# Scaling the normalised input by its rows' factors once, in place, instead of scaling the results of its projections

## Chip, core and metric

The kernel runs on one core of one Trainium2 chip. A core has TensorE (PE, the matrix engine), VectorE (DVE), ScalarE (ACT), GpSimd (POOL) and SyncE (SP, which here issues the transfers); each works through its own queue in order, and they wait for each other at semaphores. PE's results go into the banks of PSUM, 128 partitions by 512 fp32 numbers each. The metric is the device time of one execution in microseconds.

## What is computed

One layer of a decoder trunk, with 512 rows of 1024 numbers. The part that the change touches is the first norm, the projection behind it and what the projection's parts go through first:

```python
u = rms_norm(h, norm_mix_pre[l])        # h * rsqrt(mean(h*h) + EPS) * gain, row by row
proj = jnp.einsum("btd,dp->btp", u, w_in[l])
(a_x, a_gate, p_x, c_q, c_f, c_i, c_g, s_b, s_c, s_x,
 gate_logits) = jnp.split(proj, split_points, axis=-1)
y_a = rg_lru_branch(a_x, a_gate, ...)   # convolution, real-gated linear recurrence
y_b = pool_branch(p_x, ...)             # causal mean pooling over windows 2, 4, 8, 16
y_c = hgrn2_branch(c_q, c_f, c_i, c_g, ...)   # f = lb + (1 - lb) * sigmoid(c_f)
y_d = short_conv_branch(s_b, s_c, s_x, ...)   # s_b * conv3(s_c * s_x)
gates = jax.nn.sigmoid(gate_logits.reshape(bsz, t, N_BRANCHES, D_MODEL))
merged = jnp.sum(gates * branch_out, axis=2)
```

After it come an output projection, a second norm, a squared-ReLU MLP (1024 to 4096 and back) and a last norm.

## The kernel before

The input stands transposed: features on the 128 partitions, the 512 rows along the free axis, eight slices of features (k = 0 to 7). Every fp32 matmul is made of three in the format fp32r: each operand is split into a high part (ACT copies it into fp32r, L167) and a low part (DVE subtracts the high part, L168). The splits of the weights are the tiles whi and wlo (128x1024 each), those of the input uh and ul. `mm3` (L237 to L240) issues the three products: L238 high by high, L239 and L240 the mixed ones.

A slot is 256 columns of the combined projection: ten for the mixers (in the order s_c and s_x, s_b, p_x, c_f, c_q, c_i, c_g, a_x, a_gate) and 16 for the gates. `slot_mm` takes two PSUM banks and issues 48 matmuls of 128x512 into them; a unit of weights lasts for half a slot, and the weights of later units are loaded and split four units ahead, into a few buffers that come free as the matmuls that read them are done. c_i alone is computed the other way round, with rows on the partitions, in matmuls of 128x256.

The norm's gains are in uh and ul already (L266, L271). The rows' factors, 1/sqrt(mean square + EPS), are not: they are known later than PE can start. They stand along the free axis in `rstd_bc` (128x512, made on PE and copied at L371), and once more with rows on the partitions in `rst4`. So every result that leaves PSUM is multiplied by them on DVE:

```python
def evac(dst, ps):
    return dve.tensor_tensor(dst, ps, rstd_bc, ALU.mult)   # L387 is its line in the trace
```

There are 50 such products: 18 for the mixers' slots, 32 for the gates', whose sigmoid (L779) follows in place. In the names of the trace, mm and sm are banks of PSUM, t and s working tiles. The work around the change:

- s_c, s_x and s_b: product of the first two (L410), a convolution of three taps (L420, L422), times s_b (L423), split into yhi and ylo.
- p_x: the mean pooling, some ten steps on DVE (L433 to L443); its result is split (ACT's copy `t<-t` at L167, DVE's subtraction at L168), and a product with a block-diagonal matrix bd_h, bd_l follows on PE (`sm<-t,bd_h`, the pool product).
- c_f: two products, then on ACT the sigmoids of z and of -z (L466, L467).
- The first branch's gates run beside the recurrence of branch A (L560 to L597), whose functions on ACT are other ones than sigmoid; a change of function table is an ACT_TABLE_LOAD there.
- Much later a second norm's rows are transposed on PE (L910) and split into u2h and u2l, and the up projection reads them (ub).

The order of each engine's instructions isn't that of the code: a scheduler sets it when the kernel is built, except for those that the code pins. So an edit in one place can move instructions in others.

Of the kernel before, what the change touches and what calls it, by code (L numbers as in the profile page):

```python
# [9 lines left out]
F32R = mybir.dt.float32r  # L10
I32 = mybir.dt.int32
U8 = mybir.dt.uint8
AF = mybir.ActivationFunctionType
ALU = mybir.AluOpType

P = 128
T = 512
# [4 lines left out]
W = 256  # L22
# [5 lines left out]
PAD = 16  # L28
# [21 lines left out]
def tile_hybrid_trunk(ctx: ExitStack, tc: tile.TileContext, x0, xT, xn, wts, dn, par, bd, cst, msk, gains, out):  # L50
    nc = tc.nc
    act, dve, pool, pe = nc.scalar, nc.vector, nc.gpsimd, nc.tensor

    cp = ctx.enter_context(tc.tile_pool(name="cp", bufs=1))
    up = ctx.enter_context(tc.tile_pool(name="up", bufs=4))
# [6 lines left out]
    yp = mix.enter_context(tc.tile_pool(name="yp", bufs=8))  # L62
# [10 lines left out]
    def nm(s):  # L73
        cnt[0] += 1
        return f"{s}_{cnt[0]}"

    def t_tile(dt=F32):
        return tp.tile([P, 2 * TP], dt, tag="t", name=nm("t"))

    def t_full(dt=F32):  # L80
        return t_tile(dt)[:, : 2 * T].rearrange("p (c t) -> p c t", c=2)

    def t_pad():
        return t_tile().rearrange("p (c t) -> p c t", c=2)

    def s_tile(n=T):
        return sp.tile([P, T], F32, tag="s", name=nm("s"))[:, :n]

    def mm_bank():
        return mp.tile([P, T], F32, tag="mm", name=nm("mm"))  # L90
# [4 lines left out]
    def y_pair():  # L95
        r = []
        for s in ("hi", "lo"):
            r.append(yp.tile([P, 2 * T], F32R, tag="y", name=nm("y" + s)))
        return r
# [7 lines left out]
    rstd_bc = cx_.tile([P, T], F32, name="rstd_bc")  # L107
    sbd = cx_.tile([P, 3, 2, P], F32, name="sbd")
    rst4 = cp.tile([P, NT], F32, name="rst4")
# [8 lines left out]
    x0t = cx_.tile([P, T + NK], F32, name="x0t")  # L118
    xt = [ap_.tile([P, 2, T], F32, tag="acc", name=nm("xt")) for _ in range(4)]
# [46 lines left out]
    def split(hi, lo, src, pin=False):  # L166
        a_ = act.activation(hi, src, AF.Copy)  # L167
        d_ = dve.tensor_tensor(lo, src, hi.bitcast(F32), ALU.subtract)  # L168
        if pin:
            K(a_)  # L170
            K(d_)
# [59 lines left out]
    def unit():  # L231
        i = use[0]
        use[0] += 1
        prep(i + ahead[0])
        return Wt.hl.pop(i)

    def mm3(ps, lh, ll, rh, rl, first, last):  # L237
        pe.matmul(ps, lh, rh, start=first, stop=False)  # L238
        pe.matmul(ps, lh, rl, start=False, stop=False)  # L239
        pe.matmul(ps, ll, rh, start=False, stop=last)  # L240
# [10 lines left out]
            dve.tensor_tensor(t, t, h, ALU.mult)  # L251
            dve.scalar_tensor_tensor(y, t, 1.5, y, ALU.add, ALU.mult)

    uh = [up.tile([P, 4, T], F32R, tag="u", name=nm("uh")) for _ in range(2)]
    ul = [up.tile([P, 4, T], F32R, tag="u", name=nm("ul")) for _ in range(2)]

    def U(lst, k, a=0, b=T):
        return lst[k // 4][:, k % 4, a:b]

    def xhi(k):  # L260
        src = x0t[:, :T] if k == 0 else xt[k // 2][:, k % 2]
        g = x0t[:, T + k : T + k + 1]
        if k == 0:
            dve.tensor_scalar(U(uh, k), src, g, None, ALU.mult)
        else:
            act.activation(U(uh, k), src, AF.Copy, scale=g)  # L266
# [40 lines left out]
    for k in range(NK):  # L307
        pair = (0, 1) if k < 4 else (2, 3)
        if k in CUTS:
            o, e = CUTS[k]  # L310
# [62 lines left out]
    def slot_mm(bank=mm_bank, mid=None):  # L373
        bs = [bank(), bank()]
        for h in range(2):
            if h == 1 and mid:
                mid()
            wh, wl = unit()
            for kk in range(4):
                k = 4 * h + kk  # L380
                for c in range(2):
                    o = kk * W + c * P
                    mm3(bs[c], wh[:, o : o + P], wl[:, o : o + P], U(uh, k), U(ul, k), k == 0, k == NK - 1)
        return bs

    def evac(dst, ps):
        return dve.tensor_tensor(dst, ps, rstd_bc, ALU.mult)  # L387

    def emit_y(y):
        hi, lo = y_pair()  # L390
        split(hi, lo, y.rearrange("p c t -> p (c t)"))
        return (hi.rearrange("p (c t) -> p c t", c=2), lo.rearrange("p (c t) -> p c t", c=2))
# [13 lines left out]
            K(evac(sx[:, c], b1[c]))  # L406

    b2 = slot_mm(sm_bank, first_evacs)
    for c in range(2):
        dve.tensor_tensor(cx[:, c, PAD:], cx[:, c, PAD:], sx[:, c], ALU.mult)  # L410
    sb = t_full()
# [3 lines left out]
    for c in range(2):  # L415
        for j in range(SCONV):
            src = cx[:, c, PAD - (SCONV - 1) + j : PAD - (SCONV - 1) + j + T]
# [5 lines left out]
    dve.tensor_tensor(cv, cv, sb, ALU.mult)  # L423
    ys[3] = emit_y(cv)

    bs = slot_mm()
    px = t_pad()
    for c in range(2):
        dve.memset(px[:, c, :PAD], 0.0)
# [9 lines left out]
    o, _ = PAR["corr"]  # L439
# [20 lines left out]
    bs = slot_mm()  # L460
    f = t_full()
    kk_ = t_full()
    for c in range(2):
        z = s_tile()
        evac(z, bs[c])
        act.activation(f[:, c], z, AF.Sigmoid)  # L466
        act.activation(kk_[:, c], z, AF.Sigmoid, scale=-1.0)  # L467
        dve.tensor_scalar(f[:, c], f[:, c], omlb[:, c : c + 1], lb[:, c : c + 1], ALU.mult, ALU.add)
        dve.tensor_scalar(kk_[:, c], kk_[:, c], omlb[:, c : c + 1], None, ALU.mult)
    hi, lo = y_pair()  # L470
# [8 lines left out]
    bs = slot_mm()  # L479
    q = t_full()  # L480
    for c in range(2):
        evac(q[:, c], bs[c])
    vz = cx_.tile([P, NT, 2, 192], F32, name="vz")
    pool.memset(vz, 0.0)
    v = vz.rearrange("p c k (b e) -> p c k b e", e=64)[:, :, :, 0:3:2]
    uv = [unit(), unit()]
    for t in range(NT):
        if t % 2 == 0:
            vb = mm_bank()
        o = (t % 2) * W  # L490
        for k in range(NK):
            wh, wl = uv[k // 4]
            cs = slice((k % 4) * W, (k % 4) * W + W)
            mm3(vb[:, o : o + W], U(uh, k, t * P, t * P + P), U(ul, k, t * P, t * P + P),
                wh[:, cs], wl[:, cs], k == 0, k == NK - 1)
        if t % 2 == 1:
            for tt in (t - 1, t):
                dve.tensor_scalar(v[:, tt], vb[:, (tt % 2) * W : (tt % 2) * W + W].rearrange(
                    "p (k b e) -> p k b e", b=2, e=64), rst4[:, tt : tt + 1], None, ALU.mult)
    bs = slot_mm()  # L500
    sg = t_full()
    for c in range(2):
        z = s_tile()
        evac(z, bs[c])
        act.activation(sg[:, c], z, AF.Sigmoid)
        dve.tensor_tensor(sg[:, c], sg[:, c], z, ALU.mult)

    bs = slot_mm()
    ax = t_pad()
    for c in range(2):  # L510
        dve.memset(ax[:, c, :PAD], 0.0)
        evac(ax[:, c, PAD:], bs[c])
    bs = slot_mm()
    ag = t_full()
    for c in range(2):
        evac(ag[:, c], bs[c])

    ysA = y_pair()
    sTt = [yp.tile([P, 2 * T], F32, tag="y", name=nm("sT")) for _ in range(2)]
# [229 lines left out]
    def drain(*gens):  # L749
        for g in gens:  # L750
            for _ in g:
                pass
# [4 lines left out]
    def step(g):  # L757
        return next(g, True) is None
# [3 lines left out]
    def accv(d):  # L762
        return acc[d // 2][:, d % 2]

    merged = [None] * 4
    for gi, k in enumerate(GATE_ORDER):
        if gi == 2:
            drain(lru)
        if gi == 3:
            drain(hg)  # L770
        yh, yl = ys[k]
        for dh in range(2):
            gt = []
            for j in range(2):
                bs = slot_mm()
                for c in range(2):
                    g = s_tile()
                    evac(g, bs[c])
                    act.activation(g, g, AF.Sigmoid)  # L779
                    gt.append(g)  # L780
                    if gi == 0:
                        step(lru)
                    else:
                        step(hg)
                        step(hg)
                if j == 1:
                    wh, wl = unit()
                    wq = (wh, wl)
            for d4 in range(4):
                d = 4 * dh + d4  # L790
                pb = mm_bank()
                for c in range(2):
                    o = c * T + d4 * P
                    mm3(pb, wq[0][:, o : o + P], wq[1][:, o : o + P], yh[:, c], yl[:, c], c == 0, c == 1)
                if gi == 0:
                    dve.tensor_tensor(accv(d), pb, gt[d4], ALU.mult)
                else:
                    dve.tensor_tensor(gt[d4], pb, gt[d4], ALU.mult)
                    dve.tensor_tensor(accv(d), accv(d), gt[d4], ALU.add)
                if gi == 3:  # L800
                    if d % 2 == 0:
                        merged[d // 2] = y_pair()
                    mh, ml = merged[d // 2]
                    cs = slice((d % 2) * T, (d % 2) * T + T)
                    split(mh[:, cs], ml[:, cs], accv(d))
# [21 lines left out]
    for ku in range(4):  # L827
        wh, wl = unit()
        for kk in range(2):
            k = 2 * ku + kk  # L830
# [98 lines left out]
    def mid():  # L929
        tb1 = trans(1, mm_bank)  # L930
        for j in range(2):
            put(1, j, tb1[j])
# [341 lines left out]
```

## Time and profile before

| | |
|---|---|
| time, median of 3 runs | 745.71 us (745.67 to 746.75) |
| the profiled execution's own time | 746.69 us |
| its span, from the first to the last instruction | 744.9 us |
| PE busy | 736.8 us, 99% |
| DVE busy | 536.1 us, 72% |
| ACT busy | 312.8 us, 42% |
| mean granted clock of TensorE | 0.997 |

Times are microseconds from the span's start. A row of the timeline is one instruction or several of a kind in a row (x2, x4): start, time from the first's start to the last's end, engine, line, operation, result<-operands without buffer numbers; in brackets the idle time of the engine before it and what ended it. Instructions of one engine overlap a little, so that the next starts before the row's time is over.

### The profile page before, as it was taken

To read this page: it belongs to the slowest core of one execution; us is meant where nothing else is said; L and a number is where in the kernel's file an instruction comes from. 1 tells how busy PE (TensorE), PEld (TensorE's weight loads), DVE (VectorE), ACT (ScalarE), POOL (GpSimd) and SP (SyncE) were. 2 spreads that over 40 slices of the span, in tenths; PEclk is the share of its full clock that TensorE was granted. 3 is DMA by queue.
4 is the path that set the end of the run, shared out by engine and by line. 5 is a ranking of instruction groups with operands and counts; after the bars stand their busy time and mean duration, and the time that the engine had idled before them with its cause. 6 is when DMAs were issued, how large, how long until landed. Compare 5 with 4: busy or idle time off the path is not lost.

```text
span 744.9 us, 8882 instructions
## 1 busy us (share of the span) xinstructions
PE 736.8 (99%) x3506; PEld 620.4 (83%) x3506; DVE 536.1 (72%) x776; ACT 312.8 (42%) x404; POOL 7.2 (1%) x11
## 2 busy tenths in 40 slices
PE   9999999999999999999999999999999999999996
PEld 7888988888888888888888988888888888888885
DVE  6698447559997566554748785788878696976787
ACT  7424223336423322242434566544445362635322
POOL 1100000000000000000000000000000000000000
PEclk9999999999999999999999999999999999999998
DMA  9634232222222353233432614142322315030322
GB/s 333 239 100 154 85 114 85 85 85 85 84 74 97 85 184 127 88 112 94 128 109 94 259 53 170 57 141 86 118 108 90 136 58 170 0 114 29 112 86 113
DMA packets 22761, 84.59 MB, mean 114 GB/s; under 512 B 2624, under 2 KB 3520, under 8 KB 20928
## 3 DMA queue, kind: packets, MB, share of 16 engines
q1 hardware_dynamic: 22288, 83.74, 33.3%
q8 instruction: 27, 0.44, 0.3%
q10 hardware_dynamic: 432, 0.29, 0.1%
q14 instruction: 14, 0.11, 0.1%
HBM read 79.83 MB, written 4.19 MB: 113 GB/s over the span
## 4 chain that ended last, share of the span: by engine, by line
PE 97%; DVE 1%; DMA 0%; ACT 0%; issue 0%; DVEq 0%
PE mm L238 14%; PE mm L240 14%; PE mm L239 14%; PE ub L239 8%; PE ub L238 8%; PE ub L240 8%; PE db L239 6%; PE db L238 6%; PE db L240 6%; PE mm L323 3%; PE sm L612 2%; PE sm L238 2%; PE sm L240 2%; PE sm L239 2%; PE ub L1121 0%; PE ub L1120 0%
## 5 line engine op out<-in xcount | busy, mean ns | idle before, releaser
L167 ACT ACTIVATE whi<-raw 128x1024 fp32r<-128x1024 f32 x98 | 103.7, 1061 | 237.7 <-PE mm L239 109.7
L168 DVE TENSOR_TENSOR wlo<-raw,whi 128x1024 fp32r<-128x1024 f32 x98 | 119.4, 1221 | 75.7 <-ACT whi L167 75.5
L240 PE MATMUL mm<-uh,wlo 128*128 128x512 f32 x352 | 137.2, 390 | 0.0
L239 PE MATMUL mm<-ul,whi 128*128 128x512 f32 x352 | 137.1, 389 | 0.0
L238 PE MATMUL mm<-uh,whi 128*128 128x512 f32 x352 | 136.8, 390 | 0.0
L238 PE MATMUL ub<-u2h,whi 128*128 128x512 f32 (+1 forms) x288 | 105.2, 366 | 0.0
L239 PE MATMUL ub<-u2l,whi 128*128 128x512 f32 (+1 forms) x288 | 105.2, 365 | 0.0
L240 PE MATMUL ub<-u2h,wlo 128*128 128x512 f32 (+1 forms) x288 | 105.2, 365 | 0.0
L240 PEld LDWEIGHTS mm<-uh,wlo 128*128 128x128 f32 x352 | 66.1, 188 | 13.7
L239 PEld LDWEIGHTS mm<-ul,whi 128*128 128x128 f32 x352 | 66.1, 188 | 13.6
L238 PEld LDWEIGHTS mm<-uh,whi 128*128 128x128 f32 x352 | 66.1, 188 | 13.4
L238 PE MATMUL db<-fhi,ahi 128*128 128x512 f32 x196 | 76.2, 389 | 0.0
L239 PE MATMUL db<-flo,ahi 128*128 128x512 f32 x196 | 76.2, 389 | 0.0
L240 PE MATMUL db<-fhi,alo 128*128 128x512 f32 x196 | 76.2, 389 | 0.0
L240 PEld LDWEIGHTS ub<-u2h,wlo 128*128 128x128 f32 x288 | 54.3, 189 | 8.7
L238 PEld LDWEIGHTS ub<-u2h,whi 128*128 128x128 f32 x288 | 54.2, 189 | 8.8
L239 PEld LDWEIGHTS ub<-u2l,whi 128*128 128x128 f32 x288 | 54.3, 189 | 8.7
L1052 DVE TENSOR_TENSOR rows<-rows,db 128x1024 f32<-128x1024 f32 x24 | 29.2, 1217 | 23.3 <-PE db L240 23.3
L167 ACT ACTIVATE fhi<-x 128x1024 fp32r<-128x1024 f32 x28 | 29.6, 1059 | 36.6 <-PE db L240 26.6
L238 PEld LDWEIGHTS db<-fhi,ahi 128*128 128x128 f32 x196 | 36.8, 188 | 7.7
L240 PEld LDWEIGHTS db<-fhi,alo 128*128 128x128 f32 x196 | 36.8, 188 | 7.6
L239 PEld LDWEIGHTS db<-flo,ahi 128*128 128x128 f32 x196 | 36.8, 188 | 7.6
(308 smaller groups left out, 1100.9 us busy)
## 6 DMA issues: line engine op xcount, KB each, us to landing
raw<-in_wts_dram SPq DMA_DIRECT2D x102, 512.0 KB, 3.5
ab<-in_dn_dram SPq DMA_DIRECT2D x14, 1024.0 KB, 4.9
t<-in_xn_dram SPq DMA_DIRECT2D x8, 512.0 KB, 7.4
h1d<-t SPq DMA_DIRECT2D x4, 512.0 KB, 2.6
hr<-h1d SPq DMA_DIRECT2D x2, 1024.0 KB, 6.9
xt<-in_xt_dram SPq DMA_DIRECT2D x7, 256.0 KB, 5.3
out_dram<-mg SPq DMA_DIRECT2D x3, 512.0 KB, 2.6
t<-in_gains_dram SPq DMA_DIRECT2D x2, 512.0 KB, 5.9
```

The lines of the kernel that those rows point to most:

```text
L167: a_ = act.activation(hi, src, AF.Copy)
L168: d_ = dve.tensor_tensor(lo, src, hi.bitcast(F32), ALU.subtract)
L238: pe.matmul(ps, lh, rh, start=first, stop=False)
L239: pe.matmul(ps, lh, rl, start=False, stop=False)
L240: pe.matmul(ps, ll, rh, start=False, stop=last)
L323: pe.matmul(fb[s_][c], fw[pair[s_]][wi][:, o_ : o_ + P], U(us_, k), start=first and k == 0, stop=last and k == NK - 1)
L612: pe.matmul(bk[ct][:, cs].rearrange("s (h n b) -> s h n b", h=2, b=B), kk_[:, ct, cs], qo, start=True, stop=True)
L1052: dve.tensor_tensor(macc[p], macc[p], ps, ALU.add)
```

## The change

The eight slices of the unscaled input's uh and ul move to eight tiles of the pool of tiles y. After the slots s_c, s_x, s_b have been issued, a new function `scaled` multiplies the input in place by gain and rstd_bc (eight DVE instructions of 128x512) and splits it again (four ACT copies and four DVE subtractions of 128x1024) into sh and sl. p_x still reads uh and ul. From c_f on, all slots and gates read sh and sl, and their results leave PSUM without the product: the sigmoids of c_f, c_g and the gates read the bank itself, c_q, a_x and a_gate are copied by ACT, c_i by DVE, and c_g's product reads the bank.

```diff
-    uh = [up.tile([P, 4, T], F32R, tag="u", name=nm("uh")) for _ in range(2)]
-    ul = [up.tile([P, 4, T], F32R, tag="u", name=nm("ul")) for _ in range(2)]
+    uh = [yp.tile([P, 2 * T], F32R, tag="y", name=nm("uh")) for _ in range(4)]
+    ul = [yp.tile([P, 2 * T], F32R, tag="y", name=nm("ul")) for _ in range(4)]
...
     b2 = slot_mm(sm_bank, first_evacs)
+    sh = [up.tile([P, 4, T], F32R, tag="u", name=nm("sh")) for _ in range(2)]
+    sl = [up.tile([P, 4, T], F32R, tag="u", name=nm("sl")) for _ in range(2)]
+
+    def scaled(j):
+        for k in (2 * j, 2 * j + 1):
+            src = x0t[:, :T] if k == 0 else xt[j][:, k % 2]
+            dve.scalar_tensor_tensor(xt[j][:, k % 2], src, x0t[:, T + k : T + k + 1], rstd_bc, ALU.mult, ALU.mult)
+        hi, lo = (x_[j // 2][:, (j % 2) * 2 : (j % 2) * 2 + 2] for x_ in (sh, sl))
+        split(hi, lo, xt[j])
...
     ys[3] = emit_y(cv)
 
+    for j in range(4):
+        scaled(j)
     bs = slot_mm()
+    uh, ul = sh, sl
...
-        z = s_tile()
-        evac(z, bs[c])
-        act.activation(f[:, c], z, AF.Sigmoid)
-        act.activation(kk_[:, c], z, AF.Sigmoid, scale=-1.0)
+        act.activation(f[:, c], bs[c], AF.Sigmoid)
+        act.activation(kk_[:, c], bs[c], AF.Sigmoid, scale=-1.0)
...
-        evac(q[:, c], bs[c])
+        act.activation(q[:, c], bs[c], AF.Copy)
...
-                dve.tensor_scalar(v[:, tt], vb[:, (tt % 2) * W : (tt % 2) * W + W].rearrange(
-                    "p (k b e) -> p k b e", b=2, e=64), rst4[:, tt : tt + 1], None, ALU.mult)
+                dve.tensor_copy(v[:, tt], vb[:, (tt % 2) * W : (tt % 2) * W + W].rearrange(
+                    "p (k b e) -> p k b e", b=2, e=64))
...
-        z = s_tile()
-        evac(z, bs[c])
-        act.activation(sg[:, c], z, AF.Sigmoid)
-        dve.tensor_tensor(sg[:, c], sg[:, c], z, ALU.mult)
+        act.activation(sg[:, c], bs[c], AF.Sigmoid)
+        dve.tensor_tensor(sg[:, c], sg[:, c], bs[c], ALU.mult)
...
-        evac(ax[:, c, PAD:], bs[c])
+        act.activation(ax[:, c, PAD:], bs[c], AF.Copy)
...
-        evac(ag[:, c], bs[c])
+        act.activation(ag[:, c], bs[c], AF.Copy)
...
-                    evac(g, bs[c])
-                    act.activation(g, g, AF.Sigmoid)
+                    act.activation(g, bs[c], AF.Sigmoid)
```

The scheduler gives the new kernel another order. Three places show it; the numbers behind the names are tiles.

The first place is the end of c_q on PE (mm_636 before and mm_656 after are its second bank, whi_547 and whi_571 its weights, mm_714 and mm_734 c_i's bank, t_531 and t_555 the high part of the pooled tile, bd_h the block-diagonal matrix). PE's queue before:

```order
L239 MATMUL mm_636<-ul_112,whi_547 128x512
L240 MATMUL mm_636<-uh_110,wlo_548 128x512
L238 MATMUL mm_714<-whi_577,uh_109 128x256
L239 MATMUL mm_714<-wlo_578,uh_109 128x256
L240 MATMUL mm_714<-whi_577,ul_111 128x256
L238 MATMUL mm_714<-whi_577,uh_109 128x256
L238 MATMUL sm_623<-t_531,bd_h 128x512
L238 MATMUL sm_629<-t_531,bd_h 128x512
```

Here the pool product (sm) stands behind four matmuls of c_i. PE's queue at the same place after the change:

```order
L239 MATMUL mm_656<-sl_443,whi_571 128x512
L240 MATMUL mm_656<-sh_441,wlo_572 128x512
L238 MATMUL sm_643<-t_555,bd_h 128x512
L238 MATMUL sm_649<-t_555,bd_h 128x512
L238 MATMUL mm_734<-whi_601,sh_440 128x256
L239 MATMUL mm_734<-wlo_602,sh_440 128x256
L240 MATMUL mm_734<-whi_601,sl_442 128x256
L238 MATMUL mm_734<-whi_601,sh_440 128x256
```

The pool product now stands ahead of all of c_i's matmuls, right behind c_q.

The second place is the end of the pooling, on DVE and ACT (whi and wlo are splits of weights, numbered as they are used; t_520 and t_544 the pooled tile, t_531 and t_555 its high part, t_532 and t_556 its low part). DVE's queue before:

```order
L168 TENSOR_TENSOR wlo_703<-raw_641,whi_702 128x1024
L438 COPY t_520<-t_521 64x512
L440 TENSOR_TENSOR t_520<-t_520,par_s 128x2x16
L443 SCALAR_TENSOR_TENSOR t_520<-t_520,par_s,t_515 128x512 x2
L168 TENSOR_TENSOR wlo_709<-raw_671,whi_708 128x1024
L168 TENSOR_TENSOR t_532<-t_520,t_531 128x1024
```

The pooling's last steps (L440, L443) stand behind the split wlo_703 here. DVE's queue at the same place after the change (ylo_458 is branch D's, L455 and L458 are what L440 and L443 were):

```order
L168 TENSOR_TENSOR ylo_458<-t_449,yhi_457 128x1024
L453 COPY t_544<-t_545 64x512
L168 TENSOR_TENSOR wlo_839<-raw_726,whi_838 128x1024
L455 TENSOR_TENSOR t_544<-t_544,par_s 128x2x16
L458 SCALAR_TENSOR_TENSOR t_544<-t_544,par_s,t_539 128x512 x2
L168 TENSOR_TENSOR t_556<-t_544,t_555 128x1024
```

They now stand behind the split wlo_839, which is two units of weights further on. ACT's queue before:

```order
L167 ACTIVATE whi_702<-raw_641 128x1024
L167 ACTIVATE whi_708<-raw_671 128x1024
L167 ACTIVATE t_531<-t_520 128x1024
L466 ACTIVATE t_607<-s_609 128x512
L467 ACTIVATE t_608<-s_609 128x512
L466 ACTIVATE t_607<-s_615 128x512
L467 ACTIVATE t_608<-s_615 128x512
L449 ACTIVATE lbt<-lbt 128x2
L167 ACTIVATE whi_818<-raw_706 128x1024
```

The pooled tile's copy t_531 stands ahead of the four sigmoids and of whi_818 here. ACT's queue at the same place after the change (L479 and L480 are the sigmoids, which read c_f's banks mm_569 and mm_570):

```order
L167 ACTIVATE yhi_457<-t_449 128x1024
L167 ACTIVATE whi_838<-raw_726 128x1024
L167 ACTIVATE t_555<-t_544 128x1024
L479 ACTIVATE t_631<-mm_569 128x512
L480 ACTIVATE t_632<-mm_569 128x512
L479 ACTIVATE t_631<-mm_570 128x512
L480 ACTIVATE t_632<-mm_570 128x512
L495 ACTIVATE t_717<-mm_655 128x512
L495 ACTIVATE t_717<-mm_656 128x512
```

The copy t_555 now stands behind whi_838, which is the unit of weights that whi_818 was; the sigmoids still follow the copy.

The third place is ACT in the first branch's gates (s are the gates' sigmoids, mm_1349 and mm_1350 the two banks of a gate slot, L580 and L581 are L591 and L592 after, L779 is L789). ACT's queue before:

```order
L167 ACTIVATE whi_1455<-raw_1375 128x1024
L167 ACTIVATE whi_1485<-raw_1419 128x1024
L580 ACTIVATE t_1298<-t_1297 128x1024
L779 ACT_TABLE_LOAD
L779 ACTIVATE s_1401<-s_1401 128x512
L581 ACTIVATE t_1297<-t_1297 128x1024
L167 ACTIVATE whi_1565<-raw_1459 128x1024
L779 ACTIVATE s_1409<-s_1409 128x512
```

No table load stands between the slot's two sigmoids here (s_1401 and s_1409 are its two tiles); the one that there is stands between the recurrence's exponential (L580) and the first of them. ACT's queue at the same place after the change:

```order
L167 ACTIVATE whi_1463<-raw_1385 128x1024
L789 ACT_TABLE_LOAD
L789 ACTIVATE s_1411<-mm_1349 128x512
L167 ACTIVATE whi_1493<-raw_1427 128x1024
L591 ACT_TABLE_LOAD
L591 ACTIVATE t_1309<-t_1308 128x1024
L592 ACTIVATE t_1308<-t_1308 128x1024
L789 ACT_TABLE_LOAD
L789 ACTIVATE s_1418<-mm_1350 128x512
```

Two table loads stand between the slot's two sigmoids now, with the recurrence's two functions between them, and the second sigmoid reads the bank where it read a tile of SBUF before.

On PE, at the up projection, the last two groups of transposes stand two matmuls later than before.

## Rows read from the trace of the kernel before

**Rows 1.** The page, part 4: shares of the chain of waits, by engine.
```profile
PE 97%; DVE 1%; DMA 0%; ACT 0%; issue 0%; DVEq 0%
```
**Rows 2.** PE's waits, whole span: line, releaser, us in total, times, longest.
```profile
PE sm L294 <- DVE spt L567: 1.0, 1, 1.0
```
**Rows 3.** Two windows: PE, PEld, DVE, ACT, POOL busy (x instructions), PEclk, DMA, GB/s.
```profile
30.00:40.00 10.00, 10.00 (x46) 8.27 (x45) 6.60 (x10) 1.06 (x1) 0.00 (x0) 1.00 0.43 158
...
50.00:60.00 10.00, 10.00 (x46) 8.29 (x45) 9.54 (x11) 3.28 (x4) 0.00 (x0) 1.00 0.69 213
```
**Rows 4.** PE's timeline at c_q's end: start, duration, line, operation, count.
```profile
71.41 0.39 PE L240 MATMUL mm<-uh,wlo 128*128 128x512 f32 x1
71.64 0.28 PE L238 MATMUL mm<-whi,uh 128*128 128x256 f32 x1
...
72.11 0.63 PE L238 MATMUL sm<-t,bd_h 128*128 128x512 f32 x2
```
**Rows 5.** One window: from the first L410 to the end of L443.
```profile
38.92:65.91 26.99, 26.99 (x121) 22.35 (x120) 25.20 (x35) 8.17 (x8) 0.00 (x0) 1.00 0.47 145
```
**Rows 6.** DVE's timeline, in the same window and just behind it.
```profile
42.15 2.73 DVE L422 SCALAR_TENSOR_TENSOR t<-t,par_s,t 128x512 f32<-128x512 f32 x4
...
61.35 1.29 DVE L387 TENSOR_TENSOR s<-mm,rstd_bc 128x512 f32<-128x512 f32 x2
...
64.26 0.19 DVE L440 TENSOR_TENSOR t<-t,par_s 128x32 f32<-128x32 f32 x1
64.49 1.42 DVE L443 SCALAR_TENSOR_TENSOR t<-t,par_s,t 128x512 f32<-128x512 f32 x2
67.26 1.23 DVE L168 TENSOR_TENSOR wlo<-raw,whi 128x1024 fp32r<-128x1024 f32 x1 [1.36 <-ACT whi L167]
68.41 1.22 DVE L168 TENSOR_TENSOR t<-t,t 128x1024 fp32r<-128x1024 f32 x1
```
**Rows 7.** ACT's timeline around c_q's end.
```profile
66.17 1.06 ACT L167 ACTIVATE whi<-raw 128x1024 fp32r<-128x1024 f32 x1 [4.38 <-PE mm L239]
67.14 1.05 ACT L167 ACTIVATE t<-t 128x1024 fp32r<-128x1024 f32 x1
68.08 0.61 ACT L466 ACTIVATE t<-s 128x512 f32<-128x512 f32 x1
...
71.66 1.06 ACT L167 ACTIVATE whi<-raw 128x1024 fp32r<-128x1024 f32 x1 [1.30 <-issue]
```
**Rows 8.** ACT's timeline in the first branch's gates.
```profile
170.69 1.06 ACT L167 ACTIVATE whi<-raw 128x1024 fp32r<-128x1024 f32 x1 [4.38 <-PE mm L239]
171.66 1.04 ACT L580 ACTIVATE t<-t 128x1024 f32<-128x1024 f32 x1
172.72 1.28 ACT L779 ACT_TABLE_LOAD   x1
174.01 0.63 ACT L779 ACTIVATE s<-s 128x512 f32<-128x512 f32 x1
```
**Rows 9.** PE's timeline there: the next gate slot's first matmul.
```profile
176.16 0.39 PE L238 MATMUL mm<-uh,whi 128*128 128x512 f32 x1
```
**Rows 10.** DVE's timeline just before the up projection.
```profile
404.28 1.28 DVE L168 TENSOR_TENSOR u2l<-mm,u2h 128x512 fp32r<-128x512 f32 x2
```
**Rows 11.** PE's timeline: the up projection's first matmul.
```profile
405.57 0.28 PE L238 MATMUL ub<-u2h,whi 128*128 128x256 f32 x1
```
**Rows 12.** Windows behind PE's last matmul (737.74 us): see PEclk.
```profile
738.00:739.00 1.00, 0.02 (x1) 0.00 (x0) 0.96 (x5) 0.51 (x4) 0.00 (x0) 1.00 0.92 381
...
741.00:742.00 1.00, 0.00 (x0) 0.00 (x0) 0.56 (x2) 0.00 (x0) 0.00 (x0) 0.51 0.00 0
```
**Rows 13.** PE's timeline at the program's start.
```profile
1.05 3.35 PE L294 MATMUL sm<-ones 128*128 128x128 f32 x14 [1.05 <-DVE spt L567]
4.54 2.07 PE L323 MATMUL mm<-uh,whi 128*128 128x512 f32 x4
...
7.68 1.09 PE L323 MATMUL mm<-uh,wlo 128*128 128x512 f32 x4
```

## What the change is predicted to do

> **What bounds the kernel now.** I read the chain of waits first: 97% of it is PE [rows 1]. Then PE's own waits, where the reader is to see how short the list is: one wait, 1.0 us, which lies at the program's start (1.05, [rows 2, 13]). PE is never late in the middle; its 128x512 matmuls follow each other every 0.23 us (71.41 to 71.64, [rows 4]). So the kernel lasts as long as PE's matmuls are long, and what DVE and ACT do is covered as long as it arrives in time. The windows show this from the other side: PE starts 46 matmuls in 10 us where DVE is busy for 6.60 us and also where it is busy for 9.54 us [rows 3]. Work taken from DVE can therefore give nothing back by itself. Work added to DVE costs nothing either, until PE reaches a matmul whose operand isn't there. The question is only whether the change makes such a place; PE's instructions are the same in number and shape.
>
> **What goes.** 42 of the 50 products with rstd_bc go: two for c_f, c_q, c_g, a_x and a_gate each (10) and the 32 of the gates. Two of them take 1.29 us [rows 6], so some 27 us of DVE leave, nearly all of it after 75 us, where PE waits for nothing today. I cost that at nothing. The four that read PSUM with rst4 become four copies of the same shape: nothing. The ten copies that ACT gets (four halves of the scaled input, six results of c_q, a_x and a_gate) and the eight tiles of another pool for the unscaled input change no matmul; where ACT's copies stand ahead of something that PE waits for, they are in the chains below.
>
> **What comes, and where.** The order puts the eight scalings, four subtractions and four ACT copies between 39 and about 52 us, ahead of the end of slot s_b's and p_x's own work on DVE. That is the one stretch in which DVE has little to spare: from the first product of s_c and s_x (38.92 us) to the end of the pooling (L443, 65.91 us) it is busy 25.20 of 26.99 us [rows 5]. Behind this stretch stands ACT's copy t<-t, the high half of the pooled tile (67.14, 1.05 us, [rows 7]), and for that PE waits with the pool product, `sm<-t,bd_h`. Before, this matmul starts at 72.11 us [rows 4], some 3.9 us after the copy's end at 68.19. In the new order it stands four matmuls earlier: right behind c_q's last matmul, where PE arrives at 71.64 us.
>
> **When is the pooled tile ready?** Two chains lead to it, and I work out both.
>
> By the length of DVE's queue: 25.2 us of work before. Added are 8 scalings of 0.66 us (a row of four takes 2.73 us and one of two 1.42, so one more costs (2.73 - 1.42) / 2, [rows 6]), 5.3 us; 4 subtractions of 128x1024 at 1.15 us (67.26 to 68.41, [rows 6]), 4.6 us; and two more splits of weights that now stand ahead of L443's counterpart (9 wlo instead of 7), 2.3 us. Gone are c_f's two products, 1.3 us. 25.2 + 5.3 + 4.6 + 2.3 - 1.3 = 36.1 us, from 38.92 to 75.0 us.
>
> By the queue's order: ahead of the pooling's last steps DVE now has a split wlo whose whi copy is the one that ran at 71.66 us before [rows 7]. That copy goes into a buffer that c_q's matmuls read, so it can't start before PE is nearly done with c_q. It is on ACT ahead of t<-t, and its wlo is on DVE ahead of the last pooling steps. So PE waits for a chain that its own last c_q matmuls release: copy 71.66 + 1.06 = 72.72; wlo from 72.75 (0.03 behind its copy, as 67.26 stands to 66.17 + 1.06, [rows 6, 7]); the correction 1.15 later at 73.90; the two last pooling steps 0.23 later at 74.13 (64.26 to 64.49, [rows 6]), done 1.42 later at 75.55; t<-t from 75.58 to 76.63; PE at 76.66. The second chain ends last. The stop is 76.66 - 71.64 = **5.02 us**. It is a firm number, since even a DVE with nothing else to do could not shorten the second chain. Its bounds are near: 4.5 us if the queue's length alone decided (75.0 + 0.03 + 1.05 = 76.08, and the same hand-over), and 5.5 us for hand-overs of 0.1 us at five places.
>
> **The bank right behind.** After the two pool matmuls (0.46 us, 77.12) comes c_i, whose first matmul writes into the bank that c_f's first result leaves. Before, DVE's product freed it at about 62 us. Now two sigmoids on ACT read it, and they stand behind t<-t: the first 0.94 us after its start (67.14 to 68.08, [rows 7]) at 76.52, the second some 0.5 us later (0.61 us each, less 0.1 of overlap), done at 77.64. PE goes on at 77.67: **0.55 us** more. Between 0 (if the copy of c_f's bank weren't needed first) and 0.6.
>
> **The first gates.** There PE needs, 24 matmuls after the end of a gate slot, at 176.16 us [rows 9], a bank that DVE's product freed before. Now the slot's second sigmoid frees it, on an ACT that also carries the recurrence's exponentials, with a table load on each side. In the new order ACT does, from PE's release of a weight buffer at 170.69: whi 0.97, load 1.29 (172.72 to 174.01), two activations of 128x1024 2.03 (1.06 each from 171.66 to 172.72, less 0.09 of overlap), load 1.29, sigmoid 0.63 [rows 8]. 170.69 + 6.21 = 176.90, and with the hand-over PE is **0.77 us** late. Between 0 and 1.3 us (one more load). The row shows no gap around a load: the activation before it ends at 172.70, the load runs from 172.72 to 174.00, and the next starts at 174.01 [rows 8].
>
> The Trainium skill ("ScalarE: Activation LUTs", section "What ACT_TABLE_LOAD costs") puts a switch at about 1283 ns for the load and 1380 ns more for a drain. The load agrees with 1.28 us in this trace; the drain isn't in it. By the page two switches on this chain would add 2.76 us; by the row they add nothing, and the sum goes by the row.
>
> **The up projection.** Two groups of transposes stand two matmuls later than before, 0.46 us. DVE's two subtractions end at 405.56 and the first matmul of ub starts at 405.57 [rows 10, 11], so there is nothing to spare: between 0 and 0.46, I take **0.3 us**.
>
> **The clock.** Does a stop of 5 us cost more than itself? At the end of the program PE's last matmul ends at 738.02; the granted clock is still 1.00 in the window from 738 to 739 and 0.51 from 741 to 742 [rows 12], so a stop of 3 us at most lowered it from 2.4 to 1.2 GHz. The stop at 71.64 is longer. What the way back costs shows at the start: four matmuls take 2.07 us at 4.54 and 1.09 at 7.68 [rows 13], so the first speed is about half (0.53), and lasted at most from 1.05 to 7.68. An upper bound is 6.6 x 0.47 = 3.1 us, the lower one is 0 (the clock doesn't fall). I take **2.0 us**, two thirds of the bound, since the fall comes late in this stop and the start is a start from rest.
>
> The Trainium skill ("TensorE: Matmul & The Clock Gate", section "What's actually happening") says the same from the other side: throttled is the default and activity releases it. By it the clock falls in this stop; without it the sum would be 2.0 us smaller. The end of this trace agrees (0.51).
>
> **The sum.** 5.02 + 0.55 + 0.77 + 0.3 + 2.0 = 8.6 us. The profiled execution took 746.69 us, 755.3 with it; it lies 0.98 us above the median of 745.71, so the forecast for a median is 754.3 us.
>
> **The rivals.** *The clock stays up.* Everything else as above: 745.7 + 6.6 = 752.3 us. For it: the stop is broken by two matmuls and the clock needed 3 of its 5 us at the end. Against it: at the end of the program 3 us were enough [rows 12]. 0.20.
>
> *Not slower: the pooled tile arrives in time.* If ACT takes t<-t before 70.6 us, PE finds it at 71.64 and the main stop, its bank and its clock vanish; the two small stops remain, 1.1 us, and 745.7 to 746.8 us result, no change. It would need the pooling to end on DVE 5 us earlier than worked out, and the whi copy not to stand ahead. For it: DVE has 1.8 us of idle time in the stretch [rows 5]. Against it: that copy can't start before 71.66 [rows 7]. 0.04.
>
> *The tables cost more than the row says.* If ACT had to run dry at each switch, for as long again as the load itself takes (1.28 us), the first gates' stop would be 0.77 + 2 x 1.28 = 3.3 us and the time 756.9. The page named above has such a drain. For it: nothing in this trace; against it: activations follow a load within 0.02 us [rows 8]. 0.06.
>
> *The change gives what it removes.* If lighter traffic on DVE and ACT made PE's matmuls follow closer, some 27 us of DVE might buy a little; but 46 matmuls in 10 us stand at either load [rows 3]. 744 us at best, 0.02.
>
> *More than I see.* Stops at other banks that ACT now frees, of 1 to 3 us: 755.5 to 757.5. 0.08.
>
> **How the numbers follow.** The forecast has 0.60 (753 to 756), the rivals 0.20, 0.04, 0.06, 0.02 and 0.08. The range runs from 751.0 (no fall of the clock, the small terms half as large) to 756.8 (the clock's upper bound, and half a table gap). About 0.2%, 1.5 us, is what a measurement can tell from no change: faster 0.02, same 0.04, slower 0.94.
>
> **What would show it.** After: in PE's waits a new line of about 5.0 us for `sm` behind ACT's t<-t, and one of 0.5 for `mm` behind a sigmoid, both near 72 to 78 us; one of 0.8 near 182 us; the granted clock under 1.00 in windows from about 75 to 80 us; DVE's busy time some 17 us lower with no gain. Wrong if PE has no wait near 72 us, if the pool product waits under 4 us, or if the clock stays at 1.00 through the stop.

## The result, and the profile after

The changed kernel takes 756.89 us (median of four runs, 756.29 to 757.43) against 745.71 (745.67 to 746.75): 1.0144 times as long by the means of the runs, 95% interval 1.0131 to 1.0156. The prediction was 754.3 us, 751.0 to 756.8. The sign, the place and the mechanism of the main loss came as forecast; the sum missed one stop, and the median lies 0.1 us above the range's upper end, with two of the four runs under that end (756.3 and 756.4) and two over it (757.4). The profiled execution took 757.41 us, 10.72 more than that of before.

The page's first lines: busy time, share of the span, instructions.

```profile
span 755.6 us, 8861 instructions
...
PE 740.1 (98%) x3506; PEld 622.0 (82%) x3506; DVE 519.2 (69%) x746; ACT 320.8 (42%) x416; POOL 7.3 (1%) x11
```

DVE is 16.9 us less busy than before (519.2 against 536.1 us) and nothing of it came back. PE is busy 3.3 us longer with the same matmuls (740.1 against 736.8), and the other 7.4 us are new waits of PE. They answer to [rows 2]; the columns are the same.

```profile
PE sm L238 <- ACT t L167: 5.2, 1, 5.2
PE sm L623 <- DVE t L689: 1.1, 1, 1.1
PE sm L296 <- DVE spt L578: 1.1, 1, 1.1
PE mm L238 <- ACT s L789: 0.9, 1, 0.9
PE ub L238 <- DVE u2l L168: 0.2, 1, 0.2
```

Where there was one line there are five. The third is the old one. The first is the forecast's main stop: the pool product behind ACT's copy t<-t, 5.2 us where 5.02 were worked out. The fourth and fifth are the first gates and the up projection. The second, 1.1 us for the scores of branch C (sm, L623, behind DVE's L689), is one that the prediction didn't see.

ACT's timeline around the end of c_q, to be read beside [rows 7]:

```profile
71.75 1.06 ACT L167 ACTIVATE whi<-raw 128x1024 fp32r<-128x1024 f32 x1 [3.55 <-PE mm L240]
75.64 1.06 ACT L167 ACTIVATE t<-t 128x1024 fp32r<-128x1024 f32 x1 [2.84 <-DVE t L458]
76.61 0.58 ACT L479 ACTIVATE t<-mm 128x512 f32<-128x512 f32 x1
```

And DVE's, beside [rows 6]:

```profile
71.42 0.42 DVE L453 COPY t<-t 64x512 f32<-64x512 f32 x1
72.83 1.23 DVE L168 TENSOR_TENSOR wlo<-raw,whi 128x1024 fp32r<-128x1024 f32 x1 [0.99 <-ACT whi L167]
73.98 0.18 DVE L455 TENSOR_TENSOR t<-t,par_s 128x32 f32<-128x32 f32 x1
74.19 1.41 DVE L458 SCALAR_TENSOR_TENSOR t<-t,par_s,t 128x512 f32<-128x512 f32 x2
```

This is the predicted chain, step for step: the copy of weights that c_q's own matmuls release (71.75), its split on DVE (72.83, after an idle 0.99 us behind ACT), the pooling's two last steps (73.98, 74.19), the copy of the pooled tile (75.64), and then c_f's sigmoids. PE's timeline between these:

```profile
71.19 0.39 PE L240 MATMUL mm<-sh,wlo 128*128 128x512 f32 x1
76.75 1.22 PE L238 MATMUL sm<-t,bd_h 128*128 128x512 f32 x2 [5.18 <-ACT t L167]
...
78.10 0.41 PE L239 MATMUL mm<-wlo,sh 128*128 128x256 f32 x1
...
81.52 0.41 PE L240 MATMUL mm<-whi,sl 128*128 128x256 f32 x1
82.73 0.28 PE L238 MATMUL mm<-whi,sh 128*128 128x256 f32 x1
```

PE's last c_q matmul starts at 71.19 and would have been followed at 71.42; the pool product starts at 76.75. That is 5.33 us lost from start to start, of which 5.18 are idle time in the bracket. From 76.75 to 82.73 PE issues six matmuls of 128x512 and 18 of 128x256, which at the spacing of before (0.23 and 0.12 us) take 3.5 us; they took 5.98. So 2.4 us more were lost after the stop. Windows of that stretch show to what (the columns are those of [rows 3]):

```profile
74.00:75.00 1.00, 0.00 (x0) 0.00 (x0) 0.96 (x4) 0.00 (x0) 0.00 (x0) 1.00 0.00 0
75.00:76.00 1.00, 0.00 (x0) 0.00 (x0) 0.61 (x1) 0.36 (x1) 0.00 (x0) 0.52 0.49 98
...
82.00:84.00 2.00, 2.00 (x15) 1.83 (x14) 1.74 (x5) 1.27 (x2) 0.00 (x0) 1.00 0.04 8
```

The granted clock is 1.00 until 75 us, 0.52 in the next window (0.50 in those behind it), and 1.00 again from 82 us: it fell to 1.2 GHz at about 75.04, 3.5 us behind the end of PE's last matmul (71.58), and came back at about 81.9, 5.1 us after PE resumed (0.53 in the mean from 80 to 82). The 128x256 matmuls are 0.21 us apart in between (16 steps from 78.10 to 81.52) instead of 0.12. The Trainium skill ("TensorE: Matmul & The Clock Gate", section "What's actually happening") states that throttled is the default and that activity releases it. This trace agrees: half level behind the idle time, full level again with PE at work.

The stop in the first gates is the chain of table loads that was worked out from [rows 8]. ACT's timeline there:

```profile
177.79 0.60 ACT L789 ACTIVATE s<-mm 128x512 f32<-128x512 f32 x1 [2.62 <-PE mm L240]
178.29 1.05 ACT L167 ACTIVATE whi<-raw 128x1024 fp32r<-128x1024 f32 x1
179.36 1.28 ACT L591 ACT_TABLE_LOAD   x1
180.65 1.06 ACT L591 ACTIVATE t<-t 128x1024 f32<-128x1024 f32 x1
...
182.82 1.28 ACT L789 ACT_TABLE_LOAD   x1
184.12 0.60 ACT L789 ACTIVATE s<-mm 128x512 f32<-128x512 f32 x1
```

PE's matmul that waits for it:

```profile
184.77 0.50 PE L238 MATMUL mm<-sh,whi 128*128 128x512 f32 x1 [0.89 <-ACT s L789]
```

The matmul ahead of it starts at 183.49 and would have been followed at 183.72, so 1.05 us were lost from start to start, not 0.77. The chain begins where I had it: the copy starts 0.02 us behind the first of the 24 matmuls in between (178.29 and 178.27), where before it started 0.03 us ahead of that matmul (170.69 and 170.72). But it is longer, 6.43 us from 178.29 to 184.72 instead of 6.21: from the copy's start to the load 1.07 us and not 0.97, and for the two activations 2.17 and not 2.03, so the overlaps that I had taken off aren't there. Each load is followed by its activation within 0.02 us (179.36 + 1.28 = 180.64, then 180.65). The Trainium skill's drain ("ScalarE: Activation LUTs", section "What ACT_TABLE_LOAD costs") isn't in this trace either, and the rival that rested on such a gap is out.

### The profile page after: what moved, and what is told of

Same layout as the page of the kernel before. It is cut to its first block, busy times and chain, and to the rows that moved or that the text cites. A ratio compares the mean times of both kernels' runs of the same rounds, so it can differ in the third digit from the quotient of the medians.

```text
span 755.6 us, 8861 instructions
## 1 busy us (share of the span) xinstructions
PE 740.1 (98%) x3506; PEld 622.0 (82%) x3506; DVE 519.2 (69%) x746; ACT 320.8 (42%) x416; POOL 7.3 (1%) x11
## 4 chain that ended last, share of the span: by engine, by line
PE 94%; DVE 3%; ACT 1%; issue 1%; DMA 0%; DVEq 0%; ACTq 0%
PE mm L238 14%; PE mm L240 14%; PE mm L239 14%; PE ub L238 8%; PE ub L239 8%; PE ub L240 8%; PE db L238 6%; PE db L239 6%; PE db L240 6%; PE mm L325 3%; PE sm L238 2%; PE sm L239 2%; PE sm L240 2%; PE sm L623 1%; PE ub L1132 0%
## 5 line engine op out<-in xcount | busy, mean ns | idle before, releaser
L238 PE MATMUL mm<-sh,whi 128*128 128x512 f32 x336 | 130.9, 391 | 0.9 <-ACT s L789 0.9
L239 PE MATMUL mm<-sl,whi 128*128 128x512 f32 x336 | 130.9, 390 | 0.0
L240 PE MATMUL mm<-sh,wlo 128*128 128x512 f32 x336 | 130.1, 389 | 0.0
L238 PEld LDWEIGHTS mm<-sh,whi 128*128 128x128 f32 x336 | 63.1, 188 | 14.3 <-ACT s L789 1.3
L240 PEld LDWEIGHTS mm<-sh,wlo 128*128 128x128 f32 x336 | 63.1, 188 | 13.1
L239 PEld LDWEIGHTS mm<-sl,whi 128*128 128x128 f32 x336 | 63.1, 188 | 12.8
L789 ACT ACTIVATE s<-mm 128x512 f32<-128x512 f32 x32 | 19.0, 595 | 79.0 <-PE mm L240 63.2
```

The source lines that it names most:

```text
L789: act.activation(g, bs[c], AF.Sigmoid)
```

## The experiments

Eight kernels, in two series; each time stands beside runs of the kernel before on the same chip, whose median was 746.21 us in the first series and 746.49 in the second. The theory: light or heavy, DVE's load as such costs PE nothing, and each loss is a place where a result that PE waits for stands behind other work in a queue.

| kernel | us | against before, 95% interval |
|---|---|---|
| the change's gates alone | 749.51 | 1.0042 [1.0027, 1.0057] |
| the change's scaling and slots alone | 753.51 | 1.0096 [1.0080, 1.0113] |
| whole change, convolution behind the pooling | 749.46 | 1.0042 [1.0027, 1.0057] |
| whole change, the convolution's end behind the pooling | 756.08 | 1.0135 [1.0120, 1.0150] |
| whole change, convolution in the middle of the pooling | 754.98 | 1.0113 [1.0098, 1.0128] |
| convolution behind, first branch's gates copied by DVE | 746.98 | 1.0002 [0.9993, 1.0012] |
| the same with two branches' gates | 746.46 | 1.0001 [0.9992, 1.0010] |
| the same with all gates | 746.29 | 0.9997 [0.9987, 1.0006] |

### The gates alone

```diff
                     g = s_tile()
-                    evac(g, bs[c])
-                    act.activation(g, g, AF.Sigmoid)
+                    act.activation(g, bs[c], AF.Sigmoid)
```

> The kernel before with one part of the change alone: the gates' sigmoids read PSUM themselves; the input isn't scaled, so the gates' rows' factors are left out of what is computed, and 32 of the 50 products go. My theory (a stop comes only where a result that PE waits for stands behind other work): nothing at 71 us, so no fall of the clock; a stop of about 1.05 us in the first branch's gates, where the second sigmoid stands behind two table loads, and 0.4 us at the up projection; whether the 1.1 us at the scores (PE sm behind DVE's L689 in the changed kernel) come with the gates is open, I expect they do. 745.7 + 1.05 + 0.4 + 1.1 = 748.3 us; 747.2 without the scores. Rival (lighter DVE is worth something): under 745.5 us.

Measured 749.51 us, 3.3 above before. PE's waits:

```profile
PE sm L612 <- DVE t L678: 1.1, 1, 1.1
...
PE mm L238 <- ACT s L778: 0.9, 1, 0.9
PE ub L238 <- DVE u2l L168: 0.2, 1, 0.2
```

The three late stops are there, at their full size, without any scaling and with nothing at 71 us. The unseen one, at the scores, belongs to the gates. The stops come to 2.7 us from start to start (1.2, 1.05 and 0.46 in the changed kernel); the interval of the measurement, 2.0 to 4.3 us, holds that. Taking 32 products off DVE gained nothing.

### The scaling and the slots alone

```diff
                     g = s_tile()
-                    act.activation(g, bs[c], AF.Sigmoid)
+                    evac(g, bs[c])
+                    act.activation(g, g, AF.Sigmoid)
```

> The changed kernel with the gates' products put back (which scales the gates' results a second time): the scaling and the mixers' slots alone. My theory: the stop behind c_q of 5.2 us, the bank behind it and the fall of the clock are whole, 7.8 us together; the stops at the gates and the up projection are gone, and the scores' stop if it comes with the gates: 745.7 + 7.8 = 753.5 us, 754.6 if the scores' stop stays. Rival (the stops come from one another, the late ones because all is shifted): 756 to 757 us.

Measured 753.51 us, 7.3 above before. PE's waits:

```profile
PE sm L238 <- ACT t L167: 5.2, 1, 5.2
```

Only the main stop is left; the two lines left out lie in the first microseconds of the program. The rival, that the late stops follow from the shift, is out. The parts add up: 7.3 + 3.3 = 10.6 us against 10.7 between the two profiled executions.

### Less work ahead of the pooled tile, the same order behind it

Branch D's convolution is six taps, a product with s_b and a split. Here only its end goes behind the pooling:

```diff
-    dve.tensor_tensor(cv, cv, sb, ALU.mult)
-    ys[3] = emit_y(cv)
...
     split(dh_, dl_, w2[:, :, PAD:])
+    dve.tensor_tensor(cv, cv, sb, ALU.mult)
+    ys[3] = emit_y(cv)
```

> The changed kernel with only the end of branch D's convolution (the product with s_b and the split, 2.4 us of DVE) written behind the pooling's steps; nothing left out. In the new order the split of weights whose copy waits for c_q's matmuls still stands ahead of the pooling's last two steps. My theory (PE waits for a chain that its own last c_q matmuls release, copy, split, two pooling steps, copy): the stop stays at 5.2 us although DVE has 2.4 us less to do ahead: 756.9 us. Rival (the length of DVE's queue decides): the stop shrinks by 2.4 us to 2.8, the clock may then hold: 752 to 754.5 us.

Measured 756.08 us, the stop as long as in the changed kernel. The edit moved nothing that matters: in the order that the scheduler made of it, the product and the split stand between the same neighbours as in the changed kernel, ahead of the pooling's last steps (64.92 and 70.33 in DVE's timeline, 64.76 and 70.16 there). So the queue ahead of the pooled tile was not 2.4 us lighter, and the run doesn't tell the two theories apart, as it was meant to. What it shows is the chain once more:

```profile
64.92 1.22 DVE L460 TENSOR_TENSOR t<-t,t 128x1024 f32<-128x1024 f32 x1
...
70.33 1.23 DVE L168 TENSOR_TENSOR ylo<-t,yhi 128x1024 fp32r<-128x1024 f32 x1
...
72.99 1.23 DVE L168 TENSOR_TENSOR wlo<-raw,whi 128x1024 fp32r<-128x1024 f32 x1 [0.91 <-ACT whi L167]
```

DVE had come to the end of its work and idled 0.91 us for ACT's copy of weights (72.99), while PE already waited for what stands behind that split.

### The whole convolution behind the pooling

```diff
-    cv = t_full()
...
-    ys[3] = emit_y(cv)
-
     for j in range(4):
         scaled(j)
...
     split(dh_, dl_, w2[:, :, PAD:])
+    cv = t_full()
...
+    ys[3] = emit_y(cv)
```

> The changed kernel with branch D's convolution (its product, six taps, product with s_b and split) written behind the pooling's steps instead of ahead of the scaling; nothing left out. The scaling's work stays where it was. My theory: the pooled tile is done before PE needs it, so the stop of 5.2 us, the bank's stop and the fall of the clock vanish (7.8 us) and the later stops stay: 756.9 - 7.8 = 749.1 us. Rival (the scaled input itself comes too late, or some other work takes the convolution's place): a stop of over 2 us stays near 71 us, 752 us or more.

Measured 749.46 us: the main stop, the bank behind it and the fall of the clock are gone together. PE's waits, and the window of [rows 5]:

```profile
...
PE sm L623 <- DVE t L689: 1.1, 1, 1.1
PE mm L238 <- ACT s L789: 0.9, 1, 0.9
PE ub L238 <- DVE u2l L168: 0.2, 1, 0.2
```

```profile
38.92:65.91 26.99, 26.99 (x121) 22.35 (x120) 26.65 (x35) 11.53 (x12) 1.85 (x2) 1.00 0.44 141
70.00:80.00 10.00, 10.00 (x75) 9.52 (x74) 7.60 (x12) 4.46 (x7) 0.00 (x0) 1.00 0.30 98
```

All of the scaling but its first product is still in the first stretch, and DVE is busy for 26.65 of its 26.99 us, more than the 25.20 of before. (The product of s_c and s_x, which the expectation names too, stayed where it was; the rest of the convolution, some 6 us of DVE, moved.) PE doesn't wait, and the clock stays at 1.00. So the added work cost its 7.3 us only while the convolution, which nobody needs before the first gates, stood ahead of the pooling, which PE needs at 71 us. The pooled tile's copy now runs at 66.80 on ACT, ahead of the copy of weights that c_q releases:

```profile
66.80 1.07 ACT L167 ACTIVATE t<-t 128x1024 fp32r<-128x1024 f32 x1
...
71.22 1.06 ACT L167 ACTIVATE whi<-raw 128x1024 fp32r<-128x1024 f32 x1
```

### The convolution in the middle of the pooling

The same block, put between the pooling's third and fourth step.

```diff
     dve.tensor_copy(w2[64:, 0, PAD:], w4[64:, 0, PAD:])
+    cv = t_full()
...
+    ys[3] = emit_y(cv)
     dve.tensor_tensor(w2[:, 1, 7:], w4[:, 1, 7:], w4[:, 1, 3 : TP - 4], ALU.add)
```

> The changed kernel with branch D's convolution written between two of the pooling's steps; nothing left out. In the new order the split that waits for c_q's weights no longer stands ahead of the pooling's end, but the convolution's work still does: the pooled tile comes some 2 us earlier than in the changed kernel, and the stop behind c_q is 3.1 us instead of 5.2, with 0.5 us for the bank behind it. This prices the clock: it fell 3.4 us behind PE's last matmul in the changed kernel. If the clock falls all the same, 756.5 - 2.1 = 754.4 us; if it holds, another 2.2 us less, 752.2 us. I hold the second for somewhat likelier. Rival (the stop is of another origin and stays): 756.5 us.

Measured 754.98 us, 8.5 above before in its series: near the case in which the clock falls all the same (754.4), and not the one that I held for likelier. PE's waits, and windows behind the stop, in the profiled execution:

```profile
PE sm L238 <- ACT t L167: 2.8, 1, 2.8
...
```

```profile
73.00:74.00 1.00, 0.28 (x1) 0.28 (x2) 1.00 (x2) 1.00 (x2) 0.00 (x0) 0.61 0.00 0
...
78.00:80.00 2.00, 2.00 (x12) 2.00 (x11) 1.86 (x5) 0.00 (x0) 0.00 (x0) 0.50 0.04 8
80.00:82.00 2.00, 2.00 (x14) 1.82 (x14) 0.12 (x1) 0.84 (x2) 0.00 (x0) 0.99 0.00 0
```

The split of the weights that c_q releases no longer stands ahead of the pooling's end, and the stop is 2.8 us instead of 5.2. It is still a chain that PE's own last c_q matmuls release, a shorter one on ACT alone; ACT's timeline:

```profile
70.72 1.06 ACT L167 ACTIVATE whi<-raw 128x1024 fp32r<-128x1024 f32 x1 [4.38 <-PE mm L239]
71.69 1.04 ACT L167 ACTIVATE yhi<-t 128x1024 fp32r<-128x1024 f32 x1
72.63 1.04 ACT L167 ACTIVATE t<-t 128x1024 fp32r<-128x1024 f32 x1
```

Copy of weights, branch D's high part, pooled tile, one behind the other from 70.72 to 73.67; DVE was done with the pooling at 71.95. PE's timeline from there:

```profile
73.72 1.22 PE L238 MATMUL sm<-t,bd_h 128*128 128x512 f32 x2 [2.81 <-ACT t L167]
...
80.14 0.28 PE L239 MATMUL mm<-wlo,sh 128*128 128x256 f32 x1
```

The granted clock is 0.61 in the mean from 73 to 74, so it fell at about 73.2 us, 2.3 us behind PE's last matmul and half a microsecond before PE resumed at 73.72, and it was at half level until 80.0. From 73.72 to 80.14 PE issues two matmuls of 128x512 and 25 of 128x256, 3.5 us' worth at the spacing of before; they took 6.4. So in these two executions 2.9 us were lost behind the shorter stop and 2.4 behind the longer one: of the 2.4 us that the wait gave back, 0.5 went to the clock.

### Gates out of PSUM by DVE

On top of the convolution behind the pooling:

```diff
-                    act.activation(g, bs[c], AF.Sigmoid)
+                    if gi == 0:
+                        dve.tensor_copy(g, bs[c])
+                        act.activation(g, g, AF.Sigmoid)
+                    else:
+                        act.activation(g, bs[c], AF.Sigmoid)
```

> The version with branch D's convolution behind the pooling (749.5 us), and the first branch's gates copied out of PSUM by DVE, the sigmoid in place behind it, as before but without the product; nothing left out. My theory: the bank no longer waits for ACT and its table loads, so the stop of 0.9 us in the first gates goes; those at the scores (1.1) and at the up projection (0.4) stay: 748.4 us. Rival (ACT is late there whatever frees the bank): 749.5 us.

Measured 746.98 us, 0.5 above the kernel before in its series, which the interval doesn't tell from nothing; the kernel it is built on was 3.25 above, and 2.2 were expected to stay. PE's waits, without those in the first microseconds:

```profile
...
PE ub L238 <- DVE u2l L168: 0.2, 1, 0.2
```

The stop in the first gates is gone, as expected, but so is the one at the scores, although the sigmoids near it still read PSUM. So it wasn't ACT's reading there that made it, as I had it, but the order. In the kernel with the stop PE does sixteen score matmuls, thirteen of the branch projection, and then sixteen of the scores again; between the two groups DVE has a row of steps to do, from L639 to L689. DVE, and PE's second group:

```profile
202.84 1.30 DVE L639 COPY_PREDICATED sT<-msk_s,sm 128x512 f32<-128x512 uint8 x1
...
206.85 0.69 DVE L689 TENSOR_TENSOR t<-t,t 128x512 f32<-128x512 f32 x1
```

```profile
207.69 2.02 PE L623 MATMUL sm<-t,t 128*128 128x128 f32 x16 [1.05 <-DVE t L689]
```

DVE's steps begin at 202.84, right behind a split, and end at 207.54. PE issues the last of the thirteen at 206.25 and could go on at 206.48; it goes on at 207.69. With the first branch's gates copied by DVE the scheduler puts 35 matmuls between the same two groups, and the steps end at 208.79, 2.4 us before PE comes to the second group:

```profile
208.10 0.69 DVE L689 TENSOR_TENSOR t<-t,t 128x512 f32<-128x512 f32 x1
```

```profile
211.20 1.95 PE L623 MATMUL sm<-t,t 128*128 128x128 f32 x16
```

It is a choice of the scheduler, then, which the edit of the gates tipped; why it chose so, the traces don't tell, and no run sets this order by itself.

With `gi <= 1` in place of `gi == 0`:

> The same with the gates of the first two branches copied by DVE. The stop at the scores lies in the second branch, where in the changed kernel ACT's copy of weights stands behind a sigmoid that waits for PE, and DVE's split of weights behind that copy. My theory: with DVE taking these results out of PSUM that stop goes as well: 747.3 us. Rival (the scores are late because their steps stand in another order on DVE whatever the gates do): 748.4 us.

Measured 746.46 us. The scores' stop was gone already in the kernel that it is built on, so this run could no longer test what it was meant for, and neither of the two times forecast for it (747.3 or 748.4) came. With all gates copied by DVE, no condition:

> The same with all gates copied by DVE: the scaled input, 32 copies in place of 32 products. All stops should be gone: the time of the kernel before, 746.2 us within 0.5, though the scaling is in. This tells what the lighter DVE is worth to PE: nothing. Rival (the scaling's own work costs PE something): over 747.2 us.

Measured 746.29 us, as expected. PE's waits:

```profile
PE sm L296 <- DVE spt L578: 1.1, 1, 1.1
PE mm L325 <- ACT whi L313: 0.3, 1, 0.3
```

This kernel has the whole scaling, and in place of 42 products 32 copies; its DVE is busy for 539.4 us against 536.1 before. The one with two branches' copies has 528.7. Neither more nor less work on DVE shows in the time.

## Why the prediction came out as it did

- **What bounds the kernel**: right. PE's matmuls set the time. 17 us less on DVE gave nothing in the changed kernel, and the versions without the three larger stops took 746.29 to 746.98 us against 746.49, with DVE 12 us and 7 us less busy and 3 us busier than before (524.1, 528.7 and 539.4 us).
- **The main stop**: right in place, chain and size, 5.02 us forecast and 5.33 lost from start to start. The difference is the hand-over at the chain's start: PE is done with c_q 0.22 us earlier than in the trace of before (free at 71.42 for 71.64), and the copy of weights starts 0.09 us later (71.75 for 71.66), 0.33 us behind PE and not 0.02. I called the second chain firm, one that a lighter DVE could not shorten. In the order of the changed kernel the rows bear that out, since DVE idles 0.99 us in it; the run that was to test it kept the order. The chain isn't the whole of the stop, though: DVE was through with the step ahead of that split at 71.84 and began the one behind it at 73.98, so by these rows I estimate that without the split the stop would still have been about 3.2 us, from the length of DVE's queue. And the order isn't given: with the split out of the chain the stop was 2.8 us, and with the convolution behind the pooling it was none.
- **The bank behind it**: right in kind, but it took 0.2 us instead of 0.55, since the pool product's two matmuls ran at half level and covered the rest. It can't be told apart from the clock's price: 2.55 us were forecast for the two, 2.4 lost.
- **The clock**: right, 0.60 had gone to the case with its fall. That the 2.0 us came out close (2.4 with the bank) is partly luck: two thirds of the bound was a choice, while the rows show that it hangs on how much work falls in the stretch at half level. That a shorter stop costs no less of it, I had not considered.
- **The first gates**: the term 0.77 us was too small by 0.28, nearly all of it overlap between ACT's instructions that I took off and that isn't there (6.43 us of chain for 6.21). The rival with the slower tables gave 756.9 us, which is the time that was measured, but by coincidence: activations follow the loads within 0.02 us.
- **The up projection**: 0.3 forecast, 0.35 lost ahead of its first matmul and 0.1 behind it.
- **The scores**: the step that failed. The sum had nothing for it, and "More than I see" had 0.08, for stops at banks that ACT now frees; this is another kind, a chain on DVE that the new order put too close, 1.2 us. 5.33 + 2.4 + 1.05 + 0.46 + 1.2 = 10.4 us of the 10.7 between the profiled executions; without it the sum would have been 9.2 for the 8.6 forecast.
- **The sums**: two bounds don't follow from the terms named for them. With no fall of the clock and the small terms halved the lower end is 751.5 us and not 751.0, and 1 to 3 us of unseen stops give 755.3 to 757.3.

## What to carry to other kernels

Where one engine has no waits, as here, work taken from the others is worth nothing, and an edit to them can only lose; look at where their queues put what the busy engine needs next before you look at their busy time. The added scaling cost 7.3 us in one order and nothing in another, with DVE 99% busy in the stretch: before giving up a change, move what nobody needs yet behind what is needed now. A stop of the matrix engine is to be priced with its clock; in one profiled execution here 2.8 us idle cost 2.9 more.

## What was not expected of the hardware

The price of the clock didn't shrink with the stop. After 5.2 us of idle time the engine ran at 1.2 GHz for 5.1 us of work (76.75 to about 81.9), after 2.8 us for 6.3 (73.7 to 80.0); in the second case the granted clock fell only half a microsecond before PE resumed. In all four profiled executions with this stop (these two, the scaling and slots alone, and the convolution's end behind the pooling) the granted clock stood at half level for 6.8 us (75.04 to 81.87 in the changed kernel, 73.22 to 80.04 in the other); what differed was how much of that fell on PE's work.

These are single executions. In two of the four runs of the kernel with the shorter stop the mean granted clock was 0.996 and 0.997, which is too high for such a stretch, since 6.8 us at half level take 0.0045 off the mean. These runs took 754.57 and 754.75 us, the other two 755.20 and 755.35; so what a stop costs without the whole of the stretch isn't settled.

The stops of 0.9 and 1.1 us at the gates and the scores left it at full level: the kernels that have only these show a mean granted clock of 0.997, as before.
